# Preparing the last 256 output columns' weights two projections earlier, pinning the last products, and sending each finished row tile in six pieces

## The chip, the cores and the metric

The kernel runs on one core of one Trainium2 chip. TensorE (PE) multiplies matrices into PSUM; VectorE (DVE) and ScalarE (ACT) do elementwise work; GpSimd (POOL) does a few small operations; SyncE (SP) and ACT issue the DMAs used here. Each engine takes its own instructions in order and waits on semaphores for the others. The metric is device microseconds of one execution, and the time of a kernel is the median of its runs.

## The reference

A hybrid block: an HGRN2 branch and a sliding-window attention branch over 256 tokens of width 2048 (with 256 context tokens), merged by gates, projected by `w_out`, added to the input and normalised. The change concerns only the last lines, here with `y` as the merged branches:

```python
def rmsnorm(x, gain):
    xf = x.astype(jnp.float32)
    y = xf * lax.rsqrt(jnp.mean(xf * xf, axis=-1, keepdims=True) + EPS)
    return (y * gain.astype(jnp.float32)).astype(x.dtype)
...
    y = jax.nn.sigmoid(m_a + b_m[0]) * y_a + jax.nn.sigmoid(m_b + b_m[1]) * y_b
    return y @ w_out_l                       # 256 x 2048 by 2048 x 2048, float32
...
    h = h + gate * merge_and_project(...)    # gate: one row of 2048 values for all tokens
    return rmsnorm(h, final_norm_gain)
```

So each of the 256 output rows needs all its 2048 columns before its mean square is known, and only then can it be scaled and stored.

## The kernel before

**Tiles.** The 256 tokens are two row tiles of 128 (t = 0 and 1). A product over the inner width of 2048 is 16 steps (`KT`) of 128. Float32 accuracy comes from splitting both factors into a rounded part and the rest (H and L) and adding three products, one `mm3` (lines 82 to 85): three matmuls for each step and row tile.

**Weights.** `wload` (line 61) takes a tile `raw` of 128x1024 values, from a ring of four, and loads it with a DMA that SP issues (line 66). `wchunk` (line 69) calls it, then ACT makes the rounded part `wh` (line 76) and DVE the rest `wl` (line 77); both come from rings of three (lines 72 and 73), so `wh` of a chunk waits until PE has done with the chunk three before it. A load waits until `wl` of the chunk four before it is done. The two splitting steps have raised priority.

**The output projection.** Columns 0 to 1535 are three projections of 512 columns (lines 1098 to 1101): eight chunks of two inner steps each, 12 matmuls of 512 columns for a chunk. Columns 1536 to 1791 follow (lines 1103 to 1108): four chunks of four inner steps, 24 matmuls of 256 columns each. The last 256 columns (1792 to 2047) are different: their four loads stand after that, at lines 1109 to 1114; `split` (lines 883 to 885) puts the two parts into `bH` and `bL`, two large tiles that are free by then and hold all 16 steps. The products of these columns (lines 1121 to 1124) run over row tile 0 first and then over row tile 1, so that row tile 0 can be finished while PE works on row tile 1.

**What follows a projection.** `settle` (lines 1082 to 1096) multiplies by the gate row `gt` (DVE, 1087), adds the input row `xv` (DVE, 1088), squares and sums (ACT, 1091; for the last columns DVE, 1093) and multiplies by the final gain `fg` (DVE, 1096; not for the last columns). Lines 1115 to 1120 add up the sums of the first 1792 columns. After the last columns of a row tile, line 1127 adds their sum, POOL raises to the power -0.5 (1128), and the row tile is scaled in four pieces of 512 columns, two on ACT (1132) and two on DVE (1135, and 1137 with the gain for the last 256 columns). Each piece has its own DMA to `out` (1139), from ACT's queue for ACT's pieces and from SP's for DVE's.

**Order.** A scheduler orders each engine's queue by priority (program order, unless raised) and by its own estimate of when inputs are ready. Blocks under `manual_schedule` keep the named engines in program order. The output projection has no such block, so PE's products of columns 1536 to 1791 and of the last 256 columns are interleaved.

Line numbers here and L numbers in rows are the same.

Of the kernel before, what the change touches and what calls it, by code (L numbers as in the profile page):

```python
# [7 lines left out]
F32 = mybir.dt.float32  # L8
F32R = mybir.dt.float32r
U8 = mybir.dt.uint8  # L10
AF = mybir.ActivationFunctionType
ALU = mybir.AluOpType
PSUM = bass.MemoryType.PSUM

P = 128
D = 2048
T = 256
KT = D // P
# [3 lines left out]
PRIO = 100000  # L22
# [16 lines left out]
def block_kernel(ctx: ExitStack, tc: tile.TileContext, x, c, cx, c_ctx, w_ada, b_ada, norm_gain, w_in,  # L39
                 b_merge, lb_f, lb_b, hg_gain, w_oh, sink, w_oa, w_out, fin_gain, cst, msk, out):  # L40
    nc = tc.nc
    pe, act, dve, pool = nc.tensor, nc.scalar, nc.vector, nc.gpsimd

    def pl(name, bufs=1, **kw):
        return tc.tile_pool(name=name, bufs=bufs, **kw)
# [5 lines left out]
    base = ctx.enter_context(pl("base"))  # L51
# [9 lines left out]
    def wload(w, row0, nk, col0, ncol, rp=None):  # L61

        raw = (rp or wp).tile([P, 1024], F32, tag="raw", name="raw", bufs=8 if rp else 4)
        rv = raw[:, : len(col0) * nk * ncol].rearrange("p (g k c) -> p g k c", g=len(col0), k=nk)
        for g, co in enumerate(col0):
            nc.sync.dma_start(rv[:, g], w[row0: row0 + nk * P, co: co + ncol].rearrange("(k p) c -> p k c", p=P))
        return raw, rv

    def wchunk(w, row0, nk, col0, ncol):
        cl = col0 if isinstance(col0, tuple) else (col0,)  # L70
        raw, rv = wload(w, row0, nk, cl, ncol)
        h = wp.tile([P, 1024], F32R, tag="wh", name="wh", bufs=3)
        lo = wp.tile([P, 1024], F32R, tag="wl", name="wl", bufs=3)
        n = len(cl) * nk * ncol
        with tc.high_priority(PRIO):
            act.activation(h[:, :n], raw[:, :n], AF.Copy)  # L76
            dve.tensor_tensor(lo[:, :n], raw[:, :n], h[:, :n].bitcast(F32), op=ALU.subtract)  # L77
        parts = [(h[:, g * nk * ncol: (g + 1) * nk * ncol].rearrange("p (k c) -> p k c", k=nk),
                  lo[:, g * nk * ncol: (g + 1) * nk * ncol].rearrange("p (k c) -> p k c", k=nk)) for g in range(len(cl))]
        return parts if isinstance(col0, tuple) else parts[0]  # L80

    def mm3(o, s, m, first, last):
        pe.matmul(o, s[0], m[0], start=first, stop=False)  # L83
        pe.matmul(o, s[0], m[1], start=False, stop=False)  # L84
        pe.matmul(o, s[1], m[0], start=False, stop=last)  # L85

    def bank(name="pj"):
        return pj.tile([P, 512], F32, tag="pj", name=name)
# [13 lines left out]
    def result(g):  # L102

        while True:
            try:
                next(g)
            except StopIteration as e:
                return e.value

    def proj_tok(*a):  # L110
        return result(proj_tok_g(*a))
# [52 lines left out]
    mhalf = pad.tile([P, 8], F32, name="mhalf")  # L164
# [56 lines left out]
    with pl("st", reuse_waits="tile") as st:  # L221
# [11 lines left out]
        rv = lambda a: a.rearrange("(r p) -> r p", p=P)  # L233
# [236 lines left out]
    bH = hp.tile([P, KT, T], F32R, name="bH")  # L470
    bL = hp.tile([P, KT, T], F32R, name="bL")
# [411 lines left out]
    def split(dh, dl, src, **kw):  # L883
        act.activation(dh, src, AF.Copy, **kw)
        dve.tensor_tensor(dl, src, dh.bitcast(F32), op=ALU.subtract)
# [159 lines left out]
    xv = [at.tile([P, D], F32, tag=tg, name="xv") for tg in ("A", "X2")]  # L1045
    fg = [at.tile([P, 1024], F32, tag=tg, name="fg") for tg in Q_TAGS[0]]
    gt = [at.tile([P, 1024], F32, tag=tg, name="gt") for tg in Q_TAGS[1]]
# [27 lines left out]
    def y_st(kt, t):  # L1075
        sl = slice(t * P, (t + 1) * P)
        return XH[:, kt, sl], XL[:, kt, sl]

    fin = few.tile([P, 16], F32, name="fin")
    ssf = fin[:, :10].rearrange("p (t n) -> p t n", t=2)  # L1080
    rsf = fin[:, 10:12]
    def settle(t, bo, c0, width, slot, gain=True):

        cl = slice(c0, c0 + width)
        ch = slice(c0 % 1024, c0 % 1024 + width)
        ht = base.tile([P, 512], F32, tag="bb", name="ht", bufs=2)[:, :width]
        dve.tensor_tensor(ht, bo, gt[c0 // 1024][:, ch], op=ALU.mult)
        dve.tensor_tensor(xv[t][:, cl], xv[t][:, cl], ht, op=ALU.add)
        sq = base.tile([P, 512], F32, tag="sm", name="fsq", bufs=3)[:, :width]
        if gain:  # L1090
            act.activation(sq, xv[t][:, cl], AF.Square, accum_out=ssf[:, t, slot: slot + 1])
        else:
            dve.scalar_tensor_tensor(sq, xv[t][:, cl], 1.0, xv[t][:, cl], op0=ALU.mult, op1=ALU.mult,
                                     accum_out=ssf[:, t, slot: slot + 1])
        if gain:
            dve.tensor_tensor(xv[t][:, cl], xv[t][:, cl], fg[c0 // 1024][:, ch], op=ALU.mult)

    for n in range(3):
        bo = proj_tok(w_out, n * 512, y_st, range(2))
        for t in range(2):  # L1100
            settle(t, bo[t], n * 512, 512, n)

    bo = [bank() for _ in range(2)]
    for k0 in range(0, KT, 4):
        h, lo = wchunk(w_out, k0 * P, 4, D - 512, 256)
        for t in range(2):
            for j in range(4):
                mm3(bo[t][:, :256], y_st(k0 + j, t), (h[:, j, :], lo[:, j, :]), k0 + j == 0, k0 + j == KT - 1)
    for k0 in range(0, KT, 4):
        raw, _ = wload(w_out, k0 * P, 4, (D - 256,), 256)  # L1110
        rv = raw.rearrange("p (k c) -> p k c", k=4)
        ks = slice(k0, k0 + 4)
        with tc.high_priority(PRIO):
            split(bH[:, ks, :], bL[:, ks, :], rv)
    for t in range(2):
        settle(t, bo[t][:, :256], D - 512, 256, 3)

# [2 lines left out]
        dve.tensor_scalar(tot, tot, 1.0 / D, EPS, op0=ALU.mult, op1=ALU.add)  # L1120
    for t in range(2):
        be = bank()
        for kt in range(KT):
            mm3(be[:, :256], y_st(kt, t), (bH[:, kt, :], bL[:, kt, :]), kt == 0, kt == KT - 1)
        settle(t, be[:, :256], D - 256, 256, 4, False)
        rs = rsf[:, t: t + 1]
        dve.tensor_scalar(rs, ssf[:, t, 4:5], 1.0 / D, fin[:, 12 + t: 13 + t], op0=ALU.mult, op1=ALU.add)
        pool.tensor_tensor(rs, rs, mhalf[:, :1], op=ALU.pow)
        for c0, c1, on_act in ((0, 512, True), (512, 1024, False), (1024, 1536, True), (1536, D, False)):
            o_ = xv[t][:, c0: c1]  # L1130
            if on_act:
                act.activation(o_, o_, AF.Copy, scale=rs)
            else:
                e = min(c1, D - 256)
                dve.tensor_scalar(xv[t][:, c0: e], xv[t][:, c0: e], rs, None, op0=ALU.mult)
                if e < c1:
                    dve.scalar_tensor_tensor(xv[t][:, e: c1], xv[t][:, e: c1], rs, fg[1][:, e - 1024: c1 - 1024],
                                             op0=ALU.mult, op1=ALU.mult)
            (nc.scalar if on_act else nc.sync).dma_start(out[t * P: (t + 1) * P, c0: c1], o_)


def _constants():
# [50 lines left out]
```

## Time and profile before

| what | us |
|---|---|
| median of 3 runs (1636.43 to 1636.96) | 1636.56 |
| the profiled execution, whole | 1636.14 |
| its span, first to last instruction | 1634.3 |
| PE busy in the span | 1613.9 (99%) |
| DVE busy | 937.0 (57%) |
| ACT busy | 763.4 (47%) |
| POOL busy | 31.4 (2%) |

The whole execution is the span and 1.84 us around it. The profiled execution is 0.42 us below the median of the runs. PE's clock was granted at 0.997 of full speed over the span. All places in time below are microseconds from the start of the span. Busy times of consecutive instructions can overlap a little on DVE and ACT, and matmuls overlap in the pipeline, so the start-to-start distance is what a further instruction costs.

### The profile page before, as it was taken

To read this page: it belongs to the slowest core of one execution; us is meant where nothing else is said; L and a number is where in the kernel's file an instruction comes from. 1 tells how busy PE (TensorE), PEld (TensorE's weight loads), DVE (VectorE), ACT (ScalarE), POOL (GpSimd) and SP (SyncE) were. 2 spreads that over 40 slices of the span, in tenths; PEclk is the share of its full clock that TensorE was granted. 3 is DMA by queue.
4 is the path that set the end of the run, shared out by engine and by line. 5 is a ranking of instruction groups with operands and counts; after the bars stand their busy time and mean duration, and the time that the engine had idled before them with its cause. 6 is when DMAs were issued, how large, how long until landed. Compare 5 with 4: busy or idle time off the path is not lost.

```text
span 1634.3 us, 24809 instructions
## 1 busy us (share of the span) xinstructions
PE 1613.9 (99%) x9882; PEld 1329.3 (81%) x9882; DVE 937.0 (57%) x1463; ACT 763.4 (47%) x1200; POOL 31.4 (2%) x88
## 2 busy tenths in 40 slices
PE   7999999999999999999999999999999999999998
PEld 4558888888888888888888888888888888788887
DVE  4444467536665466645567455235677676555565
ACT  4333454424553345433566443224576787454443
POOL 2000000000000000000000000000000000000000
PEclk9999999999999999999999999999999999999999
DMA  9993444336343453435335555424544454665554
GB/s 356 383 384 109 142 150 149 110 127 195 104 129 117 156 176 106 131 117 177 118 119 176 186 193 193 129 90 142 179 140 146 133 168 157 231 201 192 184 191 140
DMA packets 191427, 274.89 MB, mean 168 GB/s; under 512 B 9776, under 2 KB 112592, under 8 KB 190544
## 3 DMA queue, kind: packets, MB, share of 16 engines
q1 hardware_dynamic: 189344, 268.95, 50.1%
q0 software_dynamic: 1248, 3.25, 0.7%
q8 instruction: 77, 1.26, 0.3%
q10 hardware_dynamic: 720, 1.11, 0.2%
q14 instruction: 38, 0.31, 0.1%
HBM read 271.17 MB, written 2.11 MB: 167 GB/s over the span
## 4 chain that ended last, share of the span: by engine, by line
PE 95%; DMA 2%; DVE 1%; issue 1%; ACT 0%; SPq 0%; POOLq 0%; POOL 0%; ACTq 0%
PE pj L83 24%; PE pj L85 23%; PE pj L84 23%; PE pj L141 7%; PE pj L146 4%; DMA raw<-in_w_ada_dram 2%; PE pa L306 2%; PE al L562 1%; PE pj L396 1%; PE pj L389 1%; PE sb L643 1%; PE tkp L1001 1%; PE pj L390 1%; PE oba L83 0%; PE sc L85 0%
## 5 line engine op out<-in xcount | busy, mean ns | idle before, releaser
L77 DVE TENSOR_TENSOR wl<-raw,wh 128x1024 fp32r<-128x1024 f32 x392 | 479.6, 1224 | 425.4 <-ACT wh L76 425.0
L76 ACT ACTIVATE wh<-raw 128x1024 fp32r<-128x1024 f32 x392 | 414.7, 1058 | 589.4 <-PE pj L85 428.6
L84 PE MATMUL pj<-wl,xHL 128*128 128x512 f32 (+1 forms) x1024 | 395.6, 386 | 0.4 <-DVE wl L77 0.4
L85 PE MATMUL pj<-wh,xHL 128*128 128x512 f32 (+1 forms) x1024 | 395.4, 386 | 0.0
L83 PE MATMUL pj<-wh,xHL 128*128 128x512 f32 (+1 forms) x1024 | 391.4, 390 | 0.0
L85 PEld LDWEIGHTS pj<-wh,xHL 128*128 128x128 f32 x1024 | 192.4, 188 | 39.0
L84 PEld LDWEIGHTS pj<-wl,xHL 128*128 128x128 f32 x1024 | 192.5, 188 | 38.2 <-DVE wl L77 0.7
L83 PEld LDWEIGHTS pj<-wh,xHL 128*128 128x128 f32 x1024 | 192.2, 188 | 37.8 <-DVE yt L1057 0.4
L141 PE MATMUL pj<-xHL,wh 128*128 128x512 f32 x512 | 181.1, 396 | 0.0
L83 PE MATMUL pj<-xHL,wh 128*128 128x512 f32 x416 | 164.6, 396 | 0.0
L85 PE MATMUL pj<-xHL,wl 128*128 128x512 f32 x416 | 162.1, 390 | 0.0
L84 PE MATMUL pj<-xHL,wh 128*128 128x512 f32 x416 | 162.0, 389 | 0.0
L146 PE MATMUL pj<-xHL,wl 128*128 128x256 f32 x512 | 139.9, 283 | 0.0
L141 PEld LDWEIGHTS pj<-xHL,wh 128*128 128x128 f32 x512 | 95.0, 188 | 19.2
L84 PE MATMUL pj<-wl,bH 128*128 128x512 f32 x256 | 99.9, 390 | 0.0
L85 PE MATMUL pj<-wh,bL 128*128 128x512 f32 x256 | 99.6, 389 | 0.0
L146 PEld LDWEIGHTS pj<-xHL,wl 128*128 128x128 f32 x512 | 96.7, 189 | 2.5
L85 PEld LDWEIGHTS pj<-xHL,wl 128*128 128x128 f32 x416 | 78.1, 188 | 16.7
L83 PEld LDWEIGHTS pj<-xHL,wh 128*128 128x128 f32 x416 | 78.1, 188 | 15.5
L84 PEld LDWEIGHTS pj<-xHL,wh 128*128 128x128 f32 x416 | 78.2, 188 | 15.4
L83 PE MATMUL pj<-wh,bH 128*128 128x512 f32 x256 | 89.8, 390 | 0.1
L608 DVE TENSOR_TENSOR A<-A,X 128x512 f32<-128x512 f32 x96 | 62.0, 687 | 16.7 <-ACT qk L538 6.7
(278 smaller groups left out, 1688.2 us busy)
## 6 DMA issues: line engine op xcount, KB each, us to landing
raw<-in_w_in_dram SPq DMA_DIRECT2D x292, 512.0 KB, 3.5
raw<-in_w_ada_dram SPq DMA_DIRECT2D x128, 256.0 KB, 5.5
raw<-in_w_ada_dram SPq DMA_DIRECT2D x32, 512.0 KB, 3.7
raw<-in_w_o_hgrn_dram SPq DMA_DIRECT2D x32, 512.0 KB, 3.5
raw<-in_w_o_attn_dram SPq DMA_DIRECT2D x32, 512.0 KB, 3.7
raw<-in_w_out_dram SPq DMA_DIRECT2D x32, 512.0 KB, 4.3
raw<-in_w_in_dram SPq DMA_DIRECT2D x24, 256.0 KB, 5.5
X<-in_x_dram SPq DMA_DIRECT2D x2, 1024.0 KB, 6.7
```

Source lines behind the costliest of these rows:

```text
L76: act.activation(h[:, :n], raw[:, :n], AF.Copy)
L77: dve.tensor_tensor(lo[:, :n], raw[:, :n], h[:, :n].bitcast(F32), op=ALU.subtract)
L83: pe.matmul(o, s[0], m[0], start=first, stop=False)
L84: pe.matmul(o, s[0], m[1], start=False, stop=False)
L85: pe.matmul(o, s[1], m[0], start=False, stop=last)
L141: pe.matmul(banks[i].rearrange("p (a t) -> p a t", a=2), h[:, j, cs_], xHL[:, :, kt, :T], start=kt == 0, stop=kt == KT - 1)
L146: pe.matmul(banks[i][:, :T], lo[:, j, cs_], xH[:, kt, :T], start=False, stop=False)
L306: pe.matmul(pa[32 * g: 32 * g + 32, : 2 * w], cT[:, k0 + g, :], rv_[:, :, g % nk, :], start=k0 == 0, stop=k0 == KT - 4, tile_position=(0, ...
L389: pe.matmul(o, hw, xH[:, kt, :], start=kt == 0, stop=False)
L390: pe.matmul(o, lo[:, kt - k, cs_], xH[:, kt, :], start=False, stop=False)
L396: pe.matmul(o, hw, xL[:, kt, :], start=False, stop=kt == KT - 1)
L608: dve.tensor_tensor(av, av, f.unsqueeze(3).to_broadcast([P, 2, n2, b]), op=ALU.mult)
```

## The change

The four loads of the last 256 columns move from behind the projection of columns 1536 to 1791 into the second and third projections of 512 columns: two in each, after the chunks that begin at inner steps 4 and 12 (`last_weights`). There the loaded values are also multiplied, in place, by the gate row (one DVE instruction for each load), and then split into `bH` and `bL` as before, with raised priority. So the last columns' products already contain the gate.

The last products are put under `manual_schedule` for PE. After them, and with raised priority, DVE adds the product to the input row, one `tensor_tensor_reduce` squares, scales by 1/2048 and sums, starting from the sum of the other columns, and POOL raises to the power. That drops the multiplication by the gate (1087), and line 1127.

Each row tile is scaled and stored in six pieces: DVE takes columns 0 to 255, 256 to 767 and 1792 to 2047 (SP's queue), ACT takes 768 to 1023, 1024 to 1407 and 1408 to 1791 (ACT's queue), where each DMA is issued one ACT instruction behind its piece. The sum of squares on DVE for the last columns inside `settle` goes, as does its flag `gain`.

```diff
--- before.py
+++ after.py
@@ -1079,7 +1079,7 @@
     fin = few.tile([P, 16], F32, name="fin")
     ssf = fin[:, :10].rearrange("p (t n) -> p t n", t=2)
     rsf = fin[:, 10:12]
-    def settle(t, bo, c0, width, slot, gain=True):
+    def settle(t, bo, c0, width, slot):
 
         cl = slice(c0, c0 + width)
         ch = slice(c0 % 1024, c0 % 1024 + width)
@@ -1087,31 +1087,36 @@
         dve.tensor_tensor(ht, bo, gt[c0 // 1024][:, ch], op=ALU.mult)
         dve.tensor_tensor(xv[t][:, cl], xv[t][:, cl], ht, op=ALU.add)
         sq = base.tile([P, 512], F32, tag="sm", name="fsq", bufs=3)[:, :width]
-        if gain:
-            act.activation(sq, xv[t][:, cl], AF.Square, accum_out=ssf[:, t, slot: slot + 1])
-        else:
-            dve.scalar_tensor_tensor(sq, xv[t][:, cl], 1.0, xv[t][:, cl], op0=ALU.mult, op1=ALU.mult,
-                                     accum_out=ssf[:, t, slot: slot + 1])
-        if gain:
-            dve.tensor_tensor(xv[t][:, cl], xv[t][:, cl], fg[c0 // 1024][:, ch], op=ALU.mult)
+        act.activation(sq, xv[t][:, cl], AF.Square, accum_out=ssf[:, t, slot: slot + 1])
+        dve.tensor_tensor(xv[t][:, cl], xv[t][:, cl], fg[c0 // 1024][:, ch], op=ALU.mult)
+
+    def last_weights(k0):
+
+
+        raw, _ = wload(w_out, k0 * P, 4, (D - 256,), 256)
+        rv = raw.rearrange("p (k c) -> p k c", k=4)
+        ks = slice(k0, k0 + 4)
+        with tc.high_priority(PRIO):
+            dve.tensor_tensor(rv, rv, gt[1][:, 768:].unsqueeze(1).to_broadcast([P, 4, 256]), op=ALU.mult)
+            split(bH[:, ks, :], bL[:, ks, :], rv)
 
     for n in range(3):
-        bo = proj_tok(w_out, n * 512, y_st, range(2))
+        bo = [bank() for _ in range(2)]
+        for k0 in range(0, KT, 2):
+            h, lo = wchunk(w_out, k0 * P, 2, n * 512, 512)
+            for t in range(2):
+                for j in range(2):
+                    mm3(bo[t], y_st(k0 + j, t), (h[:, j, :], lo[:, j, :]), k0 + j == 0, k0 + j == KT - 1)
+            if n and k0 in (4, 12):
+                last_weights(8 * (n - 1) + (0 if k0 == 4 else 4))
         for t in range(2):
             settle(t, bo[t], n * 512, 512, n)
-
     bo = [bank() for _ in range(2)]
     for k0 in range(0, KT, 4):
         h, lo = wchunk(w_out, k0 * P, 4, D - 512, 256)
         for t in range(2):
             for j in range(4):
                 mm3(bo[t][:, :256], y_st(k0 + j, t), (h[:, j, :], lo[:, j, :]), k0 + j == 0, k0 + j == KT - 1)
-    for k0 in range(0, KT, 4):
-        raw, _ = wload(w_out, k0 * P, 4, (D - 256,), 256)
-        rv = raw.rearrange("p (k c) -> p k c", k=4)
-        ks = slice(k0, k0 + 4)
-        with tc.high_priority(PRIO):
-            split(bH[:, ks, :], bL[:, ks, :], rv)
     for t in range(2):
         settle(t, bo[t][:, :256], D - 512, 256, 3)
 
@@ -1120,23 +1125,35 @@
         dve.tensor_scalar(tot, tot, 1.0 / D, EPS, op0=ALU.mult, op1=ALU.add)
     for t in range(2):
         be = bank()
-        for kt in range(KT):
-            mm3(be[:, :256], y_st(kt, t), (bH[:, kt, :], bL[:, kt, :]), kt == 0, kt == KT - 1)
-        settle(t, be[:, :256], D - 256, 256, 4, False)
-        rs = rsf[:, t: t + 1]
-        dve.tensor_scalar(rs, ssf[:, t, 4:5], 1.0 / D, fin[:, 12 + t: 13 + t], op0=ALU.mult, op1=ALU.add)
-        pool.tensor_tensor(rs, rs, mhalf[:, :1], op=ALU.pow)
-        for c0, c1, on_act in ((0, 512, True), (512, 1024, False), (1024, 1536, True), (1536, D, False)):
+        with tc.manual_schedule(engines={mybir.EngineType.PE}):
+            for kt in range(KT):
+                mm3(be[:, :256], y_st(kt, t), (bH[:, kt, :], bL[:, kt, :]), kt == 0, kt == KT - 1)
+        with tc.high_priority(PRIO):
+            rs = rsf[:, t: t + 1]
+            xe = xv[t][:, D - 256:]
+            dve.tensor_tensor(xe, xe, be[:, :256], op=ALU.add)
+            sq = base.tile([P, 512], F32, tag="sm", name="fsq", bufs=3)[:, :256]
+            dve.tensor_tensor_reduce(sq, xe, xe, 1.0 / D, fin[:, 12 + t: 13 + t], op0=ALU.mult, op1=ALU.add,
+                                     accum_out=rs)
+            pool.tensor_tensor(rs, rs, mhalf[:, :1], op=ALU.pow)
+        row = slice(t * P, (t + 1) * P)
+        for c0, c1 in ((0, 256), (256, 768), (1792, D)):
             o_ = xv[t][:, c0: c1]
-            if on_act:
-                act.activation(o_, o_, AF.Copy, scale=rs)
+            if c1 < D:
+                dve.tensor_scalar(o_, o_, rs, None, op0=ALU.mult)
             else:
-                e = min(c1, D - 256)
-                dve.tensor_scalar(xv[t][:, c0: e], xv[t][:, c0: e], rs, None, op0=ALU.mult)
-                if e < c1:
-                    dve.scalar_tensor_tensor(xv[t][:, e: c1], xv[t][:, e: c1], rs, fg[1][:, e - 1024: c1 - 1024],
-                                             op0=ALU.mult, op1=ALU.mult)
-            (nc.scalar if on_act else nc.sync).dma_start(out[t * P: (t + 1) * P, c0: c1], o_)
+                dve.scalar_tensor_tensor(o_, o_, rs, fg[1][:, c0 - 1024: c1 - 1024], op0=ALU.mult, op1=ALU.mult)
+            nc.sync.dma_start(out[row, c0: c1], o_)
+
+        parts = ((768, 1024), (1024, 1408), (1408, 1792))
+        with tc.manual_schedule(engines={mybir.EngineType.Activation}):
+            for z in range(4):
+                if z < 3:
+                    o_ = xv[t][:, parts[z][0]: parts[z][1]]
+                    act.activation(o_, o_, AF.Copy, scale=rs)
+                if z:
+                    cl = slice(*parts[z - 1])
+                    nc.scalar.dma_start(out[row, cl], xv[t][:, cl])
 
 
 def _constants():
```

## Rows read from the trace of the kernel before

**Rows 1.** Busy time by stretch: width, each engine's busy us (instructions), PEclk, DMA share, GB/s

```profile
1559.76:1570.64 10.88, 10.88 (x50) 9.01 (x49) 7.97 (x10) 5.58 (x8) 0.00 (x0) 1.00 0.59 196
...
1603.28:1614.80 11.52, 11.52 (x99) 11.52 (x98) 9.01 (x11) 6.94 (x10) 0.00 (x0) 1.00 0.44 140
...
1614.80:1626.40 11.60, 11.51 (x96) 11.31 (x95) 6.55 (x20) 2.79 (x7) 0.57 (x1) 1.00 0.19 72
```

**Rows 2.** Chain that ended last, 1595 to 1604: start us, us, what

```profile
1603.28 0.23 PE pj L83 x2
```

**Rows 3.** Timeline of ACT, DVE, SP: start, us, what, [idle before <- releaser]

```profile
1597.88 1.06 ACT L76 ACTIVATE wh<-raw 128x1024 fp32r<-128x1024 f32 x1 [1.66 <-PE pj L85]
...
1598.97 1.23 DVE L77 TENSOR_TENSOR wl<-raw,wh 128x1024 fp32r<-128x1024 f32 x1 [1.49 <-ACT wh L76]
...
1600.23 0.37 SPq L66 DMA_DIRECT2D raw<-in_w_out_dram  x1
...
1561.71 1.22 DVE L77 TENSOR_TENSOR wl<-raw,wh 128x1024 fp32r<-128x1024 f32 x1
...
1604.58 1.06 ACT L884 ACTIVATE bH<-raw 128x1024 fp32r<-128x1024 f32 x1 [2.92 <-DMA raw<-in_w_out_dram]
```

**Rows 4.** Line 66 (weight loads), 1500 to 1634: time to landing

```profile
DMA to landing us min/median/max: 3.4/4.0/5.5
```

**Rows 5.** Timeline of the last 8 us, second row tile (t = 1)

```profile
1626.35 0.42 DVE L1087 TENSOR_TENSOR ht<-pj,gt 128x256 f32<-128x256 f32 x1 [2.32 <-PE pj L85]
1626.81 0.42 DVE L1088 TENSOR_TENSOR xv<-xv,ht 128x256 f32<-128x256 f32 x1
1627.27 0.42 DVE L1093 SCALAR_TENSOR_TENSOR fsq<-xv 128x256 f32<-128x256 f32 x1
1627.62 0.08 DVE L1093 DVE_READ_ACCUMULATOR fsq<-xv 128x1 f32 x1
1627.73 0.21 DVE L1127 TENSOR_SCALAR fin<-fin 128x1 f32<-128x1 f32 x1
1628.03 0.56 POOL L1128 TENSOR_TENSOR fin<-fin,mhalf 128x1 f32<-128x1 f32 x1 [5.18 <-DVE fin L1127]
1628.62 1.33 ACT L1132 ACTIVATE xv<-xv,fin 128x512 f32<-128x512 f32 x2 [4.40 <-POOL fin L1128]
1628.62 0.75 DVE L1135 TENSOR_SCALAR xv<-xv,fin 128x512 f32<-128x512 f32 x2 [0.67 <-POOL fin L1128]
1629.14 0.99 SPq L1139 DMA_DIRECT2D out_dram<-xv  x2
1629.29 0.48 DVE L1137 SCALAR_TENSOR_TENSOR xv<-xv,fin,fg 128x256 f32<-128x256 f32 x1
1629.37 0.95 ACTq L1139 DMA_DIRECT2D out_dram<-xv  x2
```

**Rows 6.** Lines by form, 1540 to 1634.3: xcount | busy us, mean ns | idle before

```profile
L1135 DVE TENSOR_SCALAR xv<-xv,fin 128x512 f32<-128x512 f32 x2 | 1.0, 488 | 1.4 <-POOL fin L1128 1.4
...
L1135 DVE TENSOR_SCALAR xv<-xv,fin 128x256 f32<-128x256 f32 x2 | 0.7, 348 | 0.0
...
L1091 ACT ACTIVATE fsq<-xv 128x256 f32<-128x256 f32 x2 | 0.8, 418 | 3.0 <-DVE xv L1088 3.0
```

**Rows 7.** Busy time by half microsecond, columns as in group 1

```profile
1605.00:1605.50 0.50, 0.50 (x6) 0.50 (x5) 0.00 (x0) 0.50 (x1) 0.00 (x0) 1.00 0.96 338
...
1629.50:1630.00 0.50, 0.00 (x0) 0.00 (x0) 0.27 (x1) 0.45 (x1) 0.00 (x0) 0.50 0.07 25
...
1630.00:1630.50 0.50, 0.00 (x0) 0.00 (x0) 0.00 (x0) 0.00 (x0) 0.00 (x0) 0.50 1.02 389
...
1632.50:1633.00 0.50, 0.00 (x0) 0.00 (x0) 0.00 (x0) 0.00 (x0) 0.00 (x0) 0.50 0.39 143
```

**Rows 8.** Line 1139 (output transfers), 1626 to 1634.3: time to landing

```profile
DMA to landing us min/median/max: 2.2/3.1/3.4
```

## The prediction

> **What bounds the kernel now.** I read the granted clock first (0.997, so nothing is to be had or lost there), then the busy time by stretch, the chain that ended last, and the timeline of the queues around the change and of the last 8 us. The stretches answer the main question: while the output projection runs, PE has no gap at all. From 1559.76 to 1570.64 it is busy 10.88 of 10.88 us, in the stretch of columns 1536 to 1791 and the interleaved last columns 11.52 of 11.52, and then 11.51 of 11.60 [rows 1]. The small products begin at 1603.28 [rows 2]; there are 4 x 24 for columns 1536 to 1791 and 2 x 48 for the last columns, 192 in all, and 96 of them take 11.52 us [rows 1], 0.12 each, so they end at 1603.28 + 192 x 0.12 = 1626.32. DVE's first instruction behind them starts at 1626.35 [rows 5]. So until 1626.3 PE's own work sets the time, and behind that comes a tail of 1634.3 - 1626.3 = 8.0 us in which PE does nothing.
>
> In that tail the reader should see four links [rows 5]: DVE's multiply, add, square, accumulator read and small sum (1626.35 to 1627.94); POOL's power (1628.03 to 1628.59); scaling from 1628.62 and the first DMA issue at 1629.14; then the transfer, whose bytes flow from 1630.00 at about 390 GB/s until 1632.7 [rows 7], 1.6 us before the span ends.
>
> **Loads and splits moved.** Four SP issues, four ACT splits and four DVE subtractions leave the stretch after 1603.28 and come in earlier; four DVE multiplications of 128x1024 are new. A wait they cause today is that of ACT for the landing of one of these loads, 2.92 us before the split at 1604.58 [rows 3], with three such waits behind it that are shorter. PE was full all the while [rows 1], so removing them gives 0. What could be lost is PE time in the projections, and the cover there is this.
> - One chunk takes PE 10.88 / 4 = 2.72 us (48 of the 50 matmuls in that stretch are four whole chunks) [rows 1]. The rounded part that starts at 1597.88 is for the chunk that PE begins at 1603.28 [rows 2, 3]: three tiles of each kind are in use. Its rest is done at 1598.97 + 1.23 = 1600.20. Slack: 3.08 us.
> - The load's queue: SP issues at 1600.23, as soon as `wl` of the chunk four before is done [rows 3]; the split that needs it starts four chunks behind 1597.88, at 1608.76. The lead is 8.53 us, the landing takes 3.4 to 5.5 [rows 4]. An extra tile in the ring of four puts each load behind it one chunk later, a lead of 5.81: 0.31 to spare for the slowest landing, with the 3.08 behind it. The two extra tiles of a projection are five loads apart, so there is never more than one in the ring. Cost 0.
> - DVE: each batch adds one multiplication and one subtraction, 2 x 1.23 = 2.46 us by the nearest rows, the 128x1024 subtractions [rows 3] (the gate is read as a broadcast, of which no row here gives a price). In the first half of a projection, where the settling of the columns before lies, DVE has 7.97 of 10.88 us busy [rows 1], so 10.43 with it: nearly full, but settling has no raised priority and gives way. Today settling pushes a `wl` to 1561.71 [rows 3], 0.82 behind its usual place (1559.76 + 0.04 + 1.09 = 1560.89 by the distances of the other chunk), and PE has no gap. One multiplication ahead of it as well would make 2.05 of the 3.08. Cost 0, and if the cover is gone what lies above 3.08, for each batch.
> - ACT gets 1.06 us more in that half, 5.58 + 1.06 of 10.88. Cost 0.
>
> The multiplication adds a wait: it stands in DVE's queue until its load has landed, with `wl` of the next chunk queued behind it, for which PE waits; and ACT's split waits for it, with the next `wh` behind. That is the slower rival, below.
>
> **Last products pinned.** The same 192 matmuls without a gap end at the same 1626.32, whatever their order. In order, columns 1536 to 1791 end at 1603.28 + 96 x 0.12 = 1614.80 and the last columns of row tile 0 at 1620.56; its scaling and storing lie beside the 5.76 us of the products of row tile 1. Cost 0, gain 0.
>
> **Shorter end of a row.** The add starts at 1626.35 in the multiply's place. Start to start a 128x256 step takes 0.46 [rows 5], so the square starts at 1626.81 instead of 1627.27. `tensor_tensor_reduce` has no row; its nearest is the square with accumulator read, from 1627.27 to 1627.70, 0.43 in all. I take that: done at 1627.24. The small sum (0.21 and the gap before it) is gone; POOL starts 0.09 behind DVE as now, at 1627.33, and scaling 0.59 later, at 1627.92 instead of 1628.62: gain 0.70. Ends for the unknown instruction: 0.08 less, if it needs no separate read, to 0.42 more, if it makes two passes of a 0.42 step.
>
> **Six pieces.** The first piece on SP's queue has 256 columns instead of 512: 0.35 instead of 0.49 us [rows 6]. Done at 1628.27, issued 0.03 later, as now, at 1628.30 instead of 1629.14 [rows 5]: 0.84 earlier in all. Bytes flow 0.86 behind the first issue (1630.00 - 1629.14) [rows 5, 7], so from 1629.16. Then the others must come in time. SP's second (512 columns, 0.49) is ready about 1628.76 and its third (0.48 [rows 5]) about 1629.2. ACT's first (0.42 [rows 6]) is done at 1628.34, the second, at a width between 256 and 512 estimated as 0.57 from 0.42 and half of 1.33 [rows 5, 6], at 1628.9, the third at 1629.4; its last issue is at about 1629.45 instead of 1629.37 + 0.95 - 0.34 = 1629.98. The DMA between the second and third ACT instruction waits for a piece that is long done, and the third waits 0 for it. With 0.86 added the last bytes can start at 1630.3, while the stream needs until 1631.8 at least: transfer bandwidth sets the end, not the issues.
>
> That stream is 1.05 MB. It takes 2.5 us at full share and 0.39 / 1.02 of half a microsecond, 2.69 in all, 390 GB/s, with runs of 2 KB [rows 7]. In the new pieces 768 columns go in runs of 1 KB and 768 in runs of 1.5 KB. The nearest row for 1 KB is a weight load, 338 GB/s at a share of 0.96 [rows 7]; for 1.5 KB I take half way, 364. That costs 0.39 x (1/0.338 - 1/0.390) + 0.39 x (1/0.364 - 1/0.390) = 0.15 + 0.07 = 0.22 us. Ends: nothing, or all of the bytes at 338 GB/s, 0.42. So the end of the bytes moves by -0.84 + 0.22 = -0.62. The 1.6 us behind the last byte and the 1.84 us around the span stay.
>
> What the rows show of several transfers is that they overlap: SP issues its second only 0.66 us behind the first (0.99 for both less 0.33), while a landing takes 2.2 at least [rows 5, 8], and the bytes still flow at 389 GB/s [rows 7]. The Trainium skill, DMA: Bandwidth & Descriptors, section Bandwidth, speaks against the change: transfers should be batched to 1 MiB or more, because each has a fixed cost of some 2 us (section Anatomy of one DMA). Taken one by one on a queue, that rule would cost a queue with three pieces instead of two about 2 us more, an estimate from that page; the trace does not agree that the fixed cost adds up.
>
> **Sum.** 0 for the move, 0 for the order, -0.62 for the tail: span 1633.7, the profiled execution 1636.14 - 0.62 = 1635.52. The median of the runs is 0.42 above the profiled execution, so 1636.56 - 0.62 = 1635.94, say 1635.9. With the ends of the two unknown prices (-0.08 to +0.42; -0.22 to +0.20) the change is -0.92 to 0.00, 1635.6 to 1636.6; with the scatter of the runs shown, -0.13 and +0.40 about the median, 1635.5 to 1637.0.
>
> **Rivals.**
> - *Slower: the new multiplications hold up PE.* Place: DVE's queue in the second and third projections. If the scheduler's estimate of the landing is too early, the multiplication is queued ahead of a `wl` and waits for its load. That the estimate can be too early is shown by ACT's 2.92 us [rows 3]. That wait and the multiplication delay `wl` by 2.92 + 1.22 = 4.14, 1.06 over the slack of 3.08; with split and subtraction ahead too (1.06 + 1.23), 6.43, 3.35 over. Four batches: 4.2 to 13.4 us, less 0.6: 1640.2 to 1649.3. It decides from a delay of 3.08 on. Against it: these loads are issued early, into a tile that was free anyway, and land about as long ahead as the loads beside them, which no split waits for. A milder form, one or two batches over, gives 1637 to 1639.8.
> - *The pieces go one by one.* One more transfer on each queue, at the shortest landing of 2.2 [rows 8], less the 0.84: 1636.56 + 1.36 = 1637.9. Against it, the overlap above. (The page of the Trainium skill named above, with its fixed cost for each transfer, speaks for it.)
> - *Faster: ACT's waits did cost PE time.* One wait of 2.92 given back, with the 0.62: 1633.0. Against it, PE's 11.52 of 11.52 [rows 1].
>
> **How the numbers follow.** Forecast 0.80, milder hold-ups 0.05, pieces one by one 0.05, PE held up 0.08, faster 0.02. A measurement of this kernel can tell about 0.2%, 3.3 us, from no change: within it lie the first three, 0.90; slower 0.08; faster 0.02. The range from 1635.2 to 1638.0 takes in the forecast's own range and the one-by-one case; it leaves out the hold-ups and the faster case.
>
> **What would show it.** Right: PE busy all of 1540 to 1626.3 and its last product at about 1626.3; the POOL power at 1627.3; first output issue at 1628.3; bytes flowing from 1629.2 to 1632.1, below 390 GB/s. Wrong: idle time of PE released by `wl` in the second or third projection, a DVE multiplication that waits for a load with `wl` behind it, a `tensor_tensor_reduce` of 0.8 us or more, or gaps in the transfers of the last pieces.

## The result, and the profile after

The median after is 1640.42 us (1638.66 to 1641.25, 13 runs) against 1636.75 before (1636.38 to 1637.87, 13 runs): a ratio of 1.0021, 95% interval 1.0013 to 1.0029. The change makes the kernel 3.7 us slower. It was forecast at 1635.9, in a range that ended at 1638.0.

The profiled execution after took 1640.93 us with a span of 1639.0, 4.7 us more than the one before. Three parts make up the 4.7: the start, the output projection and the end.

**The start.** The two executions differ already where the programs do not. Line 396 belongs to the first products, up to some 135 us into the span. The rows are its weight loads: number, duration of one in ns (least, median, greatest), then when the first and the last of them start. First the kernel before:

```profile
L396 PEld LDWEIGHTS pj<-xHL,wh x64: 186/188/192, 42.8 to 135.3; 128*128 128x128 f32 x64
```

The same group in the changed kernel:

```profile
L396 PEld LDWEIGHTS pj<-xHL,wh x64: 186/188/190, 44.2 to 137.2; 128*128 128x128 f32 x64
```

And in one of the experiments below (e5), which has the same program lines up to there:

```profile
L396 PEld LDWEIGHTS pj<-xHL,wh x64: 186/188/190, 42.7 to 135.8; 128*128 128x128 f32 x64
```

The changed kernel is 1.9 us late at that point. A finer event is the first transposition of line 1061 after 1540, before and after:

```profile
1542.77 0.60 PE L1061 MATMUL tky<-cs,y 128*128 128x128 f32 x4
...
1544.56 0.60 PE L1061 MATMUL tky<-cs,y 128*128 128x128 f32 x4
```

By it the changed kernel is 1.79 us late. The experiment e5 is 0.77 late there, others 0.13 to 1.91; in most of them the greater part is there by line 396. Executions of one and the same kernel differ as much: the 33 runs of the kernel before that were made beside e1 to e4 go from 1635.56 to 1638.19 us. So I read this part as scatter between executions and not as the change; in what follows it is taken off.

**The output projection.** Busy time by stretch, after; the columns are those of [rows 1].

```profile
1559.76:1570.64 10.88, 10.88 (x49) 9.01 (x49) 10.15 (x12) 6.40 (x10) 0.00 (x0) 1.00 0.71 213
...
1581.52:1592.40 10.88, 9.61 (x41) 7.31 (x41) 8.11 (x10) 5.71 (x9) 0.00 (x0) 1.00 0.57 192
1592.40:1603.28 10.88, 9.83 (x44) 7.78 (x43) 7.81 (x9) 4.65 (x5) 0.00 (x0) 1.00 0.60 192
```

PE was full in the stretches of [rows 1]; now 1.27 and 1.05 us are missing from two stretches of the third projection. That is the idle time the profile shows. The loss itself is larger. PE's last product, before and after:

```profile
1626.03 0.28 PE L85 MATMUL pj<-bH,xHL 128*128 128x256 f32 x1
...
1631.07 0.28 PE L85 MATMUL pj<-bH,xHL 128*128 128x256 f32 x1
```

It ends at 1631.35 instead of 1626.31, 5.04 later, of which 1.79 is the start. **3.25 us** are lost in the projection. The waits between 1540 and 1620 say for whom (total, times, longest):

```profile
ACT bH L884 <- DVE raw L1100: 11.4, 4, 4.6
...
DVE raw L1100 <- DMA raw<-in_w_out_dram: 10.1, 4, 3.5
ACT wh L76 <- DMA raw<-in_w_out_dram: 5.1, 3, 1.9
...
PEld pj L84 <- DVE wl L77: 3.6, 3, 1.5
PE pj L84 <- DVE wl L77: 2.3, 3, 1.1
```

The four multiplications (line 1100) waited 10.1 us for their loads, and ACT's four splits behind them 11.4 us. Ordinary loads came late too: ACT's rounding (line 76) waited for three of them, 1.9 us at most, where the kernel before shows no such wait. PE and its weight loads waited for `wl`. DVE's queue shows how the one leads to the other:

```profile
1559.40 1.23 DVE L1100 TENSOR_TENSOR raw<-raw,gt 128x1024 f32<-128x1024 f32 x1 [0.93 <-DMA raw<-in_w_out_dram]
1560.54 1.22 DVE L77 TENSOR_TENSOR wl<-raw,wh 128x1024 fp32r<-128x1024 f32 x1
...
1572.54 1.23 DVE L1100 TENSOR_TENSOR raw<-raw,gt 128x1024 f32<-128x1024 f32 x1 [2.63 <-DMA raw<-in_w_out_dram]
1573.68 1.22 DVE L77 TENSOR_TENSOR wl<-raw,wh 128x1024 fp32r<-128x1024 f32 x1
...
1584.29 1.22 DVE L1100 TENSOR_TENSOR raw<-raw,gt 128x1024 f32<-128x1024 f32 x1 [3.50 <-DMA raw<-in_w_out_dram]
1585.43 1.22 DVE L77 TENSOR_TENSOR wl<-raw,wh 128x1024 fp32r<-128x1024 f32 x1
...
1597.86 1.23 DVE L1100 TENSOR_TENSOR raw<-raw,gt 128x1024 f32<-128x1024 f32 x1 [3.07 <-DMA raw<-in_w_out_dram]
1599.00 1.22 DVE L77 TENSOR_TENSOR wl<-raw,wh 128x1024 fp32r<-128x1024 f32 x1
```

Each multiplication stands directly ahead of a `wl` of line 77, and waits for its own load first: 0.93, 2.63, 3.50 and 3.07 us. The last three of these `wl` stand in the kernel before at:

```profile
1569.05 1.23 DVE L77 TENSOR_TENSOR wl<-raw,wh 128x1024 fp32r<-128x1024 f32 x1 [1.45 <-ACT wh L76]
...
1579.93 1.23 DVE L77 TENSOR_TENSOR wl<-raw,wh 128x1024 fp32r<-128x1024 f32 x1 [1.49 <-ACT wh L76]
...
1590.81 1.23 DVE L77 TENSOR_TENSOR wl<-raw,wh 128x1024 fp32r<-128x1024 f32 x1 [1.45 <-ACT wh L76]
```

With the 1.79 of the start taken off, the changed kernel has them 2.84, 3.71 and 6.40 us later. The slack that the prediction worked out was 3.08. The second batch stays within it, the third goes over it, and the 6.40 of the fourth is 3.32 above it, which is the loss of 3.25 but for 0.07.

These are PE's rows with idle time ahead of them; each is the second product of a step, the one that needs `wl`:

```profile
1586.70 0.50 PE L84 MATMUL pj<-wl,xHL 128*128 128x512 f32 x1 [0.22 <-DVE wl L77]
...
1590.77 0.50 PE L84 MATMUL pj<-wl,xHL 128*128 128x512 f32 x1 [1.05 <-DVE wl L77]
...
1600.27 0.50 PE L84 MATMUL pj<-wl,xHL 128*128 128x512 f32 x1 [1.05 <-DVE wl L77]
```

The first and the third wait for the `wl` behind a multiplication (1585.43, 1599.00). The second waits for the `wl` at 1589.50, which stands behind four steps of settling and splitting: its rounded part was done at 1587.56, but DVE, with no idle time since the multiplication at 1584.29, worked through what was queued ahead of it.

One turn of the chain of waits, shortened: the load that the fourth multiplication needs was issued only when an earlier `wl` was done.

```profile
1591.32 1.15 DVE wl L77
...
1592.48 5.28 DMA raw<-in_w_out_dram
...
1597.86 0.06 DVE raw L1100
```

A `wl` ends, which frees a tile of the ring; the load into that tile takes 5.28 us; the multiplication waits for it; the next `wl` (1599.00) stands behind the multiplication; PE waits for that (1600.27).

**The end.** The rows that answer to [rows 5], from PE's last product at 1631.35 on:

```profile
1631.38 0.42 DVE L1134 TENSOR_TENSOR xv<-xv,pj 128x256 f32<-128x256 f32 x1 [2.98 <-PE pj L85]
1631.84 0.48 DVE L1136 CUSTOM_DVE_ANT_0 fsq<-xv,fin 128x256 f32<-128x256 f32 x1
1632.25 0.08 DVE L1136 DVE_READ_ACCUMULATOR2_ANT fin<- 128x1 f32 x1
1632.41 0.56 POOL L1138 TENSOR_TENSOR fin<-fin,mhalf 128x1 f32<-128x1 f32 x1 [5.18 <-DVE fin L1136]
1633.01 1.01 ACT L1153 ACTIVATE xv<-xv,fin 128x256 f32<-128x256 f32 x2 [4.19 <-POOL fin L1138]
1633.01 0.75 DVE L1143 TENSOR_SCALAR xv<-xv,fin 128x256 f32<-128x256 f32 x2 [0.67 <-POOL fin L1138]
1633.39 1.31 SPq L1146 DMA_DIRECT2D out_dram<-xv  x3
1633.55 0.34 ACTq L1156 DMA_DIRECT2D out_dram<-xv  x1
...
1634.05 0.86 ACTq L1156 DMA_DIRECT2D out_dram<-xv  x2
```

Scaling starts 1.66 us behind PE's last product instead of 2.31, and the first issue 2.04 instead of 2.83 behind it. The bytes, in quarters of a microsecond (columns as before):

```profile
1634.25:1634.50 0.25, 0.00 (x0) 0.00 (x0) 0.00 (x0) 0.25 (x1) 0.00 (x0) 0.50 1.00 356
...
1636.75:1637.00 0.25, 0.00 (x0) 0.00 (x0) 0.00 (x0) 0.00 (x0) 0.00 (x0) 0.50 0.90 332
1637.00:1637.25 0.25, 0.00 (x0) 0.00 (x0) 0.00 (x0) 0.00 (x0) 0.00 (x0) 0.50 0.08 25
```

They begin 2.91 us behind PE's last product (before: 3.68), flow for 2.72 us (2.70) and end at 5.63 (6.38). The end is taken where the full rate stops; the 25 GB/s of the last row are left out, here and below. But from the last byte to the end of the span it is now 2.02 us instead of 1.61. So the end as a whole is 7.65 us instead of 7.99: a gain of 0.34.

The sum: 1.79 + 3.25 - 0.34 = 4.70, the difference of the spans.

One part lies outside of the spans. The time of a run less its span is 1.78 us for the kernel before and 2.01 for the changed one, as means over the runs. It is 1.94 to 2.14 in every kernel below with six pieces, and 1.77 in the one with four (e6), which differs from e3 (1.94) in the pieces alone. Of the 3.7 us between the medians 3.25 - 0.34 = 2.91 is thus in the span and 0.23 around it; I put the 0.5 that is left to the scatter of the start.

### The profile page after: what moved, and what is told of

It reads as the page before. It is cut to its first block, busy times and chain, and to the rows that moved or that the text cites. A ratio compares the mean times of both kernels' runs of the same rounds, so it can differ in the third digit from the quotient of the medians.

```text
span 1639.0 us, 24819 instructions
## 1 busy us (share of the span) xinstructions
PE 1616.5 (99%) x9882; PEld 1329.6 (81%) x9882; DVE 939.5 (57%) x1463; ACT 763.2 (47%) x1202; POOL 31.3 (2%) x88
## 3 DMA queue, kind: packets, MB, share of 16 engines
q0 software_dynamic: 1248, 3.25, 0.8%
HBM read 271.17 MB, written 2.11 MB: 167 GB/s over the span
## 4 chain that ended last, share of the span: by engine, by line
PE 89%; DMA 8%; DVE 2%; issue 1%; ACT 0%; POOLq 0%; POOL 0%; SPq 0%; DVEq 0%; ACTq 0%
PE pj L83 23%; PE pj L84 23%; PE pj L85 22%; PE pj L141 7%; DMA raw<-in_w_ada_dram 5%; PE pj L146 4%; PE al L562 1%; DMA raw<-in_w_out_dram 1%; DVE wl L77 1%; PE sb L643 1%; PE tkp L1001 1%; DMA raw<-in_w_in_dram 1%; PE oba L83 0%; DMA X<-in_x_dram 0%; PE sc L85 0%
```

## The experiments

Theory: the multiplications wait for their loads in DVE's queue, with `wl` behind them, and PE loses what exceeds its slack of about 3 us. Rivals: DVE has too much to do; the multiplication itself is too long; the end of the kernel or the order of the last products costs the time; the late start belongs to the change. In the table, "late" is the event at 1542.77 of before, "lost" is the end of PE's last product less 1626.31 and less that lateness, and the last four columns count from PE's last product.

| kernel | median us | ratio to before (95%) | late | lost by PE | end of span | first bytes | last bytes | then |
|---|---|---|---|---|---|---|---|---|
| before | 1636.8 | | 0 | 0 | 7.99 | 3.68 | 6.38 | 1.61 |
| after | 1640.42 | 1.0021 (1.0013 to 1.0029) | 1.79 | 3.25 | 7.65 | 2.91 | 5.63 | 2.02 |
| e1, old place | 1638.28 | 1.0009 (1.0000 to 1.0018) | 1.54 | 0.00 | 9.05 | | 6.55 | 2.50 |
| e2, own tiles, tied | 1637.12 | 1.0003 (0.9994 to 1.0012) | 0.13 | 0.00 | 8.26 | 2.91 | 5.62 | 2.64 |
| e3, own tiles | 1636.23 | 0.9998 (0.9989 to 1.0007) | 1.91 | 0.01 | 7.67 | 2.90 | 5.61 | 2.06 |
| e4, no gate | 1639.14 | 1.0014 (1.0005 to 1.0023) | 1.68 | 0.87 | 8.74 | 3.36 | 6.09 | 2.65 |
| e5, two batches | 1636.87 | 1.0002 (0.9993 to 1.0011) | 0.77 | 0.00 | 7.72 | 2.91 | 5.61 | 2.11 |
| e6, four pieces | 1636.56 | 0.9997 (0.9989 to 1.0006) | 1.42 | 0.01 | 7.36 | 3.03 | 5.71 | 1.65 |
| e7, the end alone | 1637.68 | 1.0005 (0.9996 to 1.0014) | 0.30 | 0.01 | 8.68 | 3.37 | 6.09 | 2.59 |

Each median is of 11 runs (13 for the change); e1 to e4 shared their runs of before (1636.80, 33 runs), and so did e5 to e7 (1636.82, 27 runs).

### e1: the move undone

```diff
-            if n and k0 in (4, 12):
-                last_weights(8 * (n - 1) + (0 if k0 == 4 else 4))
...
+    for k0 in range(0, KT, 4):
+        last_weights(k0)
     for t in range(2):
         settle(t, bo[t][:, :256], D - 512, 256, 3)
```

> Undoes the move alone: the four loads, multiplications and splits stand behind the projection of columns 1536 to 1791 again; pinned products, the shorter end and the six pieces stay. Theory (the multiplications wait for their loads in the second and third projections and hold up PE by 3.25 us): no wait of PE for wl between 1540 and 1603, the time from PE's last product to the end stays at 7.65 us, and the kernel is 0.3 us below the one before, about 1636.4. Rival (the tail or the pinned order costs the time): it stays near 1640. Second rival (what was late by 1.8 us at 1540 in the profiled execution of the changed kernel belongs to the change): 1638 or more.

PE lost nothing, as the theory has it: the hold-up goes with the move. But the time was 1638.28, above the theory's and below the first rival's, and the end of the span is 9.05 us behind PE's last product. The time alone would also fit the second rival (1638 or more), and this execution was 1.54 late at 1542.77. Against that rival: e2 and e5, which have the same program lines for the first 1400 us, were 0.13 and 0.77 late, and e3, 1.91 late in its profiled execution of 1637.85, has a median of 1636.23. The lateness goes with the execution. DVE's queue, first row tile and second row tile:

```profile
1625.97 0.42 DVE L1134 TENSOR_TENSOR xv<-xv,pj 128x256 f32<-128x256 f32 x1 [2.73 <-PE pj L85]
...
1628.28 0.41 DVE L1134 TENSOR_TENSOR xv<-xv,pj 128x256 f32<-128x256 f32 x1
```

The first row tile's last product is added at 1625.97, the second's at 1628.28, 2.3 us apart; before, the second was added at 1626.35 [rows 5] and the first at 1620.59, 5.75 us apart. The second row tile's 48 products take 5.76 us, so 2.3 us between the ends means that products of the second row tile ran between those of the first, although the block that pins them was there. A likely reason, not tried by itself: with the multiplications the last weights are done later at this place (the fourth `bL` starts at 1620.37, before at 1615.25). The bytes of the first row tile then run straight into those of the second. Of the 1.4 us that this end takes more than that of the changed kernel, 0.9 are in the stream and 0.5 behind it. What follows: this run is no clean measure of the end.

### e2: the same work without the wait

```diff
+    early = []
+    for i, (po, tg, nb) in enumerate(((fp, "F0", 2), (fp, "F0", 2), (fp, "F1", 1), (hp, "vc", 1))):
+        rv_ = po.tile([P, 2, 512], F32, tag=tg, name="early", bufs=nb).rearrange("p a c -> p (a c)")
+        rv_ = rv_.rearrange("p (k c) -> p k c", k=4)
+        nc.sync.dma_start(rv_, w_out[4 * i * P: 4 * (i + 1) * P, D - 256: D].rearrange("(k p) c -> p k c", p=P))
+        early.append(rv_)
...
-            dve.tensor_tensor(rv, rv, gt[1][:, 768:].unsqueeze(1).to_broadcast([P, 4, 256]), op=ALU.mult)
+            one = fin[:, 14 + k0 // 8: 15 + k0 // 8]
+            if k0 % 8 == 0:
+                dve.tensor_scalar(one, ssf[:, 0, k0 // 8: k0 // 8 + 1], 0.0, 1.0, op0=ALU.mult, op1=ALU.add)
+            dve.scalar_tensor_tensor(rv, rv, one, gt[1][:, 768:].unsqueeze(1).to_broadcast([P, 4, 256]), op0=ALU.mult,
+                                     op1=ALU.mult)
```

> Takes away what the multiplications wait for, not the work: the four loads go to tiles of their own, well ahead, and each multiplication also takes a factor 1.0 that exists only when the settling of the projection before has summed its squares, so none stands in DVE's queue before its load has landed. DVE has the same four multiplications and subtractions in the same two projections, even two of each close together. Theory (waiting for the landing is the cause): DVE waits 0 for these loads, PE waits 0 for wl, about 1636.4. Rival (DVE is too full with 2.4 us more for a batch): PE still loses about 3 us, 1639 to 1640.

The waits between 1540 and the end that bear on it (total, times, longest):

```profile
DVE wl L77 <- ACT wh L76: 17.1, 13, 1.5
```

The list has no wait of DVE for a load and none of PE for `wl`; PE lost 0.00. DVE did the same four multiplications and subtractions in the same two projections, two of each close together. So the work is not the cause; the wait for the landing is. The run also takes the four loads out of the ring, so ACT's waits for ordinary loads are gone with it; the chain above shows that PE's time was lost behind the multiplications' loads and not behind those. The median is 0.7 us above what was expected; in the profiled execution that lies in the end (8.26 us; see e7), not in the projection.

### e3: own tiles alone

The same as e2 without the factor `one`: the loads go early into tiles of their own, the multiplications stand where the scheduler believes the loads to have landed (most of them ahead of the projections of 1536 columns then, since the loads are early).

> Half of the run before: the loads go to tiles of their own and no longer depend on the ring, but the multiplications stand where the scheduler believes the loads to have landed. Theory A (a load that is issued late, behind wl of a late chunk, is the cause): DVE waits for these loads under 1 us each, PE 0, about 1636.4. Theory B (the scheduler's estimate of a landing is always too early): DVE waits 1 to 3 us for each as in the changed kernel; whether PE waits depends on the slack of 3.08 us, 1636.4 to 1638.

From 1540 on DVE waited for none of these loads, PE lost 0.01, and the median is 1636.23, where theory A had it. But three of the four multiplications stand before 1540 here, and each of those did wait:

```profile
1441.07 1.23 DVE L1099 TENSOR_TENSOR early<-early,gt 128x1024 f32<-128x1024 f32 x1 [1.46 <-DMA early<-in_w_out_dram]
...
1489.39 1.23 DVE L1099 TENSOR_TENSOR early<-early,gt 128x1024 f32<-128x1024 f32 x1 [0.75 <-DMA early<-in_w_out_dram]
...
1534.12 1.23 DVE L1099 TENSOR_TENSOR early<-early,gt 128x1024 f32<-128x1024 f32 x1 [0.74 <-DMA early<-in_w_out_dram]
```

So theory B has a part too: the multiplication came ahead of its load's landing in tiles of their own as well, by 0.74 to 1.46 us, against 0.93 to 3.50 for loads that hang on the ring, where the issue waits for a `wl` that is itself late. These shorter waits cost PE nothing: this execution was 2.0 us late at line 396 and 1.91 at 1542.77. Because the multiplications also stand elsewhere, e3 does not part the ring from the place; e2, at the old place, does away with the wait altogether.

### e4: the moved batches without the multiplication

```diff
-            dve.tensor_tensor(rv, rv, gt[1][:, 768:].unsqueeze(1).to_broadcast([P, 4, 256]), op=ALU.mult)
...
-            dve.tensor_tensor(xe, xe, be[:, :256], op=ALU.add)
+            ht = base.tile([P, 512], F32, tag="bb", name="ht", bufs=2)[:, :256]
+            dve.tensor_tensor(ht, be[:, :256], gt[1][:, 768:], op=ALU.mult)
+            dve.tensor_tensor(xe, xe, ht, op=ALU.add)
```

> Drops the multiplication of the weights from the moved batches and puts the multiplication of the product by the gate back into the end of a row; loads and splits stay moved. Theory (the wait for the landing is the cause): the wait passes to ACT's rounding of these weights, with the next wh behind it, 2 to 3 us each; wl is late by that less 1.2, PE loses 0 to 1.5 us, the end of a row costs 0.46 more: 1636.8 to 1638.3. Rival (the 1.2 us of the multiplication are the cause): no wait for the landing of over 1 us anywhere, PE loses 0, 1636.9.

Waits from 1540 on:

```profile
ACT bH L884 <- DMA raw<-in_w_out_dram: 11.5, 4, 4.0
...
PE pj L84 <- DVE wl L77: 0.6, 1, 0.6
```

The wait moved to ACT, 11.5 us for the four splits, and PE still lost 0.87 us. So the rival (the 1.2 us of the multiplication as the cause) falls: the wait stays without it. But the multiplication is a good part of the price: with it in the queue the loss is 3.25. The median of 1639.14 lies above the expected 1638.3; the end of this kernel took 8.74 us, 0.6 more than the 0.46 for the multiply would make of the 7.65 (see e7).

### e5: two batches instead of four

```diff
-            if n and k0 in (4, 12):
+            if n == 1 and k0 in (4, 12):
...
-                mm3(be[:, :256], y_st(kt, t), (bH[:, kt, :], bL[:, kt, :]), kt == 0, kt == KT - 1)
+                mm3(be[:, :256], y_st(kt, t), (bH[:, kt % 8, :], bL[:, kt % 8, :]), kt == 0, kt == KT - 1)
```

> The changed kernel without the two batches of the third projection (their loads, multiplications and splits are left out, and the last products use the first half of the weights twice, so the values differ); the two batches of the second projection stay as they are. Theory (PE loses only what the delay of wl has above the slack of about 3 us): the multiplications of the second projection wait 0.9 and 2.6 us again, PE does not wait for wl, and the kernel is 0.3 us below the one before: 1636.4. Rival (each batch costs PE about a quarter of the 3.25 us): PE loses 1.6 us, 1638.

DVE's queue, the two multiplications and the `wl` behind each:

```profile
1558.39 1.22 DVE L1100 TENSOR_TENSOR raw<-raw,gt 128x1024 f32<-128x1024 f32 x1 [0.95 <-DMA raw<-in_w_out_dram]
1559.54 1.22 DVE L77 TENSOR_TENSOR wl<-raw,wh 128x1024 fp32r<-128x1024 f32 x1
...
1571.43 1.23 DVE L1100 TENSOR_TENSOR raw<-raw,gt 128x1024 f32<-128x1024 f32 x1 [2.54 <-DMA raw<-in_w_out_dram]
1572.58 1.22 DVE L77 TENSOR_TENSOR wl<-raw,wh 128x1024 fp32r<-128x1024 f32 x1
```

They waited 0.95 and 2.54 us, and PE lost 0.00. A delay of `wl` up to there is free. In the changed kernel the first two waits are as long (0.93 and 2.63) and PE shows no idle time behind them either; all of its waits come behind the third and fourth, 3.50 and 3.07, which meet a DVE queue that is already late. The median of 1636.87 is not to be told from before.

### e6: four pieces

The kernel of e3 with the four pieces of 512 columns of before.

> The kernel of the run with own tiles, but with the four pieces of 512 columns of before; early loads, folded gate and the short end of a row stay. The six pieces were to start the bytes 0.14 us earlier and to slow them by 0.22. Theory: bytes start 3.0 us behind PE's last product instead of 2.9, flow for 2.7 us, and the kernel is within 0.3 us of the one with six pieces, 1636.2 to 1636.5. Rival (more transfers mean a longer way from the last byte to the end): the time from the last byte to the end falls from 2.0 to 1.6 us, 1635.9.

The bytes began 0.13 us later than in e3, flowed for 2.68 us, and the way from the last byte to the end fell from 2.06 to 1.65: the end of the span is 0.31 us earlier against PE's last product. Both theory and rival had a part right. By the runs the two kernels (1636.56 and 1636.23) can't be told apart.

### e7: the end alone on the kernel before

The one-instruction square and sum and the six pieces, put into the kernel before; loads, splits, and the multiply by the gate as before.

> The kernel before, its loads and splits in their old place and without the folded gate, with the one-instruction square and sum and the six pieces alone. PE's products are in the order of before. The multiply by the gate stays in the end of a row, so of the 0.70 us only 0.24 are had, and 0.14 from the first piece, less the slower bytes. Theory: PE ends where it ended, bytes start 0.35 us earlier against PE's last product, the kernel is within 0.3 us of the one before, 1636.6 to 1637.0. Rival (the pieces cost time at the end): 0.4 us or more above it.

PE ended where it ended, and the bytes began 0.31 us earlier against PE's last product. Yet the span ends 0.69 later, and the median is 1637.68, as the rival had it (0.86 above, though the interval takes in no change). The transfers of the last 7.3 us say where (GB/s in 40 slices, then one of the queues):

```profile
GB/s 0 0 0 0 0 0 0 0 0 0 62 376 365 376 444 410 337 370 371 404 368 379 424 373 390 256 6 17 25 25 17 0 0 0 0 0 0 0 0 0
...
q14 instruction: 1, 0.01, 0.4%
```

Behind the main stream 6 to 25 GB/s go on for 0.9 us. A sixteenth of the full 390 GB/s is 24, so I read this as one of the 16 DMA engines that ends late; the rows don't tell the engines apart. In the same stretch there is one packet of an instruction queue (q14). The profiled executions of e1, e2, e4 and e7 have that packet among the last stores and such a tail of 0.7 to 0.9 us; in before, after, e3 and e6 it falls 9.5 us or more ahead of the stores of the second row tile, in e5 there is none in the last 20 us of the span, and none of these five has the tail.

## Why the prediction was wrong

- *PE bounds the kernel, the move can gain nothing in the projections, the order of the last products neither.* Right: in every run but the changed kernel and e4 PE's last product stands within 0.01 us of its old place, once the start is taken off, with the block that pins (e2, e3, e5) and without it (e7).
- *Loads and splits moved: cost 0.* Wrong; 3.25 us. The step that failed is the sentence in the slower rival that these loads "land about as long ahead as the loads beside them, which no split waits for". The lead of 8.53 us [rows 3] is had by ordinary loads because their split waits for PE, three chunks back. Nothing holds a moved batch back except its landing. My reading of the queues, not of the scheduler itself: it is queued where the landing is expected, with no lead. All four multiplications waited in the changed kernel (10.1 us), two of two in e5 and three of four in e3. The prediction worked out the lead of the loads behind the new ones (5.81 us) and not that of the new ones. The 5.81 was not enough either: landings between 1540 and 1604 reached 5.8 us, and ACT waited for ordinary loads up to 1.9 us, in e5 up to 1.8; that alone cost PE nothing (e5), since the slack of 3.08 lies behind it.
- *The ring.* I let the extra load take a tile that was "free anyway". The trace shows its issue at the end of a `wl` like all others, and landings of 3.53, 4.86, 5.78 and 5.28 us in the chain, against a median of 4.0 [rows 4]. A late `wl` makes the next load late, and that load the next multiplication: the waits grew from 0.93 to 3.50.
- *The rival's mechanism and place were right* (DVE's queue, a `wl` behind the multiplication, the estimate too early, deciding from 3.08 us on), its chance of 0.08 was far too low, and its price, 4.2 to 13.4 us, too high. It took each of four batches as over the slack and added them up; two were over it, and the loss is what the latest `wl` has above the slack. That the median of 1640.42 lies in its range, which begins at 1640.2, is partly luck: the loss of 3.25 lies below the 4.2, and the time around the span and the start made up for it. The upper end of the milder form, 1639.8, does not follow from its prices: at 3.35 us a batch, one makes 1639.3 and two 1642.6.
- *DVE is nearly full, but its cover holds.* Right for the work: e2 does the same there without loss. That settling "gives way" was wrong: at 1587.56 it was queued ahead of a `wl` that could have begun, and this `wl` started at 1589.50.
- *The shorter end.* Right in its first part: `tensor_tensor_reduce` took 0.48 us and a read of 0.08, against a taken 0.43 in all and an upper end of 0.92. Scaling started 0.65 us earlier against PE's last product (predicted 0.70), the bytes 0.77 (0.84).
- *Six pieces.* The price of short runs, 0.22 us, was not there: 2.72 us against 2.70. Instead the way from the last byte to the end grew by 0.41, which I had taken as fixed. So the tail gained 0.34 instead of 0.62; e6 ties the 0.41 to the number or size of the pieces (1.65 with four). The time around the span, taken as fixed at 1.84, grew as well, by 0.23, and e6 ties that to the pieces too. Together that leaves 0.11 of the 0.62. Why the last landing is seen later was not tried. The one-by-one rival is refuted by the same rows.
- *The median.* With the hold-up taken away it is 1636.23 (e3) or 1637.12 (e2), 0.3 and 1.2 above the forecast of 1635.9, and neither is to be told from before: the forecast of "same" held for the change without its hold-up, and whether any of the 0.62 was gained these runs can't show.

What stays open: the profiled executions differ by up to 1.9 us before the programs differ, and I didn't try why; the medians carry some of it.

## What to carry to other kernels

A load that is moved ahead is only early if its buffer is. If it goes through the ring that it shares with the critical loads, its issue hangs on their progress, and whatever consumes it at once stands in an in-order queue ahead of the work that PE waits for. Give it a buffer that is free long before (e2, at the same place: no wait and nothing lost by PE; e3: 1636.23 instead of 1640.42), let its consumer wait for something later than the landing, as in e2, and for each step put into a busy queue ask two leads: that of the work behind it, and its own.

## What the runs showed that I had not expected

- One packet of an instruction queue among the last stores goes with a tail of 0.7 to 0.9 us at about a sixteenth of the full rate; four of the nine profiled executions have both, and five have neither. Where the packet falls differs between kernels that differ by a few instructions. That it is the cause was not tried by itself.
- Six output pieces, three quarters of their bytes in runs of 1 and 1.5 KB, streamed as fast as four pieces in runs of 2 KB (1.05 MB in 2.72 against 2.70 us), while a stretch of weight loads in runs of 1 KB had shown 338 GB/s [rows 7].
- At 1542.77 of the kernel before, the other eight profiled executions were 0.13 to 1.91 us late, which is up to three times the whole gain that was at stake. In most of them the greater part arises in the first 120 us, where the transfers are at full share.
